# Grouping the 512-wide and the 256-wide matmuls of a turned product in a decoder block

## The chip, the cores and the metric

The kernel runs on one core of one Trainium2 chip. The metric is the device time in microseconds of one execution. Before the change it is 2248.23 us, the median of three runs (2248.22 to 2249.44).

## What is computed

One decoder block on 256 tokens of 2048 features, in float32: a half-step SwiGLU feed-forward net (5632 hidden features), a mixing stage with retention heads and sliding-window heads, cross-attention into 256 memory tokens, a second half-step feed-forward net and a final norm. Cut to what matters:

```python
h = h + 0.5 * swiglu(rms_norm(h, g1), w_gate1, w_up1, w_down1)
n = rms_norm(h, gm) @ w_in                      # queries, keys, values, gates
h = h + concat(retention(n), sliding_window(n)) @ w_out
h = h + cross_attention(rms_norm(h, gx), rms_norm(mem, gme), wq, wkv, wo)
h = h + 0.5 * swiglu(rms_norm(h, g2), w_gate2, w_up2, w_down2)
out = rms_norm(h, gf)
# swiglu(x, g, u, d) = (silu(x @ g) * (x @ u)) @ d
```

Nearly all of the work is the products with weight matrices.

## The kernel before

**Products in halves.** Every float32 operand of a product is written as the sum of a high and a low half in the format `fp32r` (the helper `halves`, lines 70 to 73: ScalarE copies the high half, VectorE subtracts it to get the low one). A product is then three products of halves: high by high, high by low, low by high.

**Two kinds of product.** A plain product holds 128 tokens in TensorE's array and streams 512 (once 256) weight columns past them: `by_tokens` (lines 196 to 203) issues three matmuls per tile of 128 rows through `three` (lines 359 to 363), all of one width. A *turned* product holds a 128x128 tile of the weights in the array and streams the tokens: `by_weights` (lines 205 to 215). Its inputs are blocks `x` of `[128, 4, 2, 256]`: four tiles of 128 features, each as its high and its low half for 256 tokens. For one tile `k` and one half `f` of the unit's 256 output columns it issues two matmuls. The wide one (line 214) holds the weights' high half and streams both halves of `x` in one pass of 512 columns. The narrow one (line 215) holds the weights' low half and streams the high half of `x`, 256 columns, into the first 256 columns of the same bank. Each matmul has a weight load of its own. `acc` is `[128, 2, 512]`: the index `f` chooses one of two banks.

**The stream.** All weight products stand in one list of units (`Unit`, line 129), each a group of 256 or 512 output columns; `run_stream` (line 171) cuts them into steps. A step of a turned product is one block of 512 rows: 4 tiles x 2 halves x 2 matmuls, 16 matmuls. The feed-forward gate and up products, the first down product, the retention queries and keys, `w_out` and cross-attention's queries, keys and output are turned. The other products are plain. A unit of 2048 rows has four turned steps; the units of the first down product have six and five. The first step of a unit opens its accumulation (`start`), the last one closes it (`stop`); in the last tile of the last step the narrow matmul goes first (lines 211 and 212), so that the wide one closes the bank.

**What sets the order.** The instructions are written out step by step. Before each step `run_due` issues small tasks that fell due (norms, attention scores, transposes), and `prepare` keeps the weights three steps ahead (`LOOKAHEAD`, line 30): SyncE issues the load of two steps' weights at once into one of three buffers (`load`, line 147), ScalarE makes the high half `wh` and VectorE the low half `wl` (`split`, line 152) in one of four buffers each. The first eight steps alternate between two units, and their loads are issued ahead of the loop. When a unit's last step is through, its `done` function reads the accumulator.

Of the kernel before, what the change touches and what calls it, by code (L numbers as in the profile page):

```python
# [17 lines left out]
P = 128  # L18
S = 256
# [18 lines left out]
def decoder_block(ctx: ExitStack, tc: tile.TileContext, a: dict, out: bass.AP):  # L38
    nc = tc.nc
# [14 lines left out]
    def blk(dt=F32R):  # L54
        """Four tiles of 128 features by 256 tokens, each as its high and its low half."""
        return work.tile([P, 4, 2, S], dt, tag="blk", name=nm("blk"), bufs=13)
# [13 lines left out]
    def halves(hi, lo, src):  # L70
        """src as the exact sum of two short halves."""
        copy(hi, src)
        nc.vector.tensor_tensor(lo, src, hi, ALU.subtract)  # L73
# [18 lines left out]

    # ------------------------------------------------------------------
    # The stream of weight products, with small tasks between its steps.
    # A product either holds the tokens in the array and gives [tokens, 512 columns], or (turned)
    # holds the weights in it and gives [256 columns, tokens], as two parts still to be added.
    st = {}
    units = []
    tasks = []
# [5 lines left out]
    def when(ready, delay, fn):  # L105
        """fn after a delay, and once ready() holds."""
        def attempt():
            if ready():
                fn()
            else:  # L110
                later(1, attempt)
        later(delay, attempt)
# [16 lines left out]
    class Unit:  # L129
        """One group of n output columns of a product with w, laid out in pieces of 1024 per partition."""  # L130

# [5 lines left out]
        def steps(self):  # L137
            """(unit, block, its tiles of 128 rows, piece of w, first, last)"""
            per = 1024 // self.n
            out = [  # L140
                (self, b, range(i * per, (i + 1) * per), b * (4 // per) + i)
                for b in self.blocks
                for i in range(4 // per)
            ]
            return [x + (i == 0, i == len(out) - 1) for i, x in enumerate(out)]
# [13 lines left out]
    def pin():  # L159
        """Keeps each engine's instructions so far in the order in which they were written."""  # L160
        prev = {}
        for ins in nc.cur_bb.bb.instructions:
            if ins.engine in prev:
                tc.add_manual_dep(
                    ins, prev[ins.engine].name,
                    mybir.DependencyInfo(mybir.DependencyClass.NoSync, mybir.DependencyReason.DATA),
                    reason="program order",
                )
            prev[ins.engine] = ins

    def run_stream():
# [24 lines left out]
        def by_tokens(u, acc, x, wh, wl, ks, t, first, last):  # L196
            ts = slice(t * P, (t + 1) * P)
            o = acc[:, t, : u.n]
            for i, k in enumerate(ks):
# [3 lines left out]
                )  # L203

        def by_weights(acc, x, wh, wl, first, last):
            for k in range(4):
                for f in range(2):
                    fs = slice(f * P, (f + 1) * P)
                    both, main = acc[:, f, :], acc[:, f, :S]
                    if last and k == 3:  # L210
                        nc.tensor.matmul(main, wl[:, k, fs], x[:, k, 0, :], start=False, stop=False)  # L211
                        nc.tensor.matmul(both, wh[:, k, fs], x[:, k, :, :], start=False, stop=True)  # L212
                    else:
                        nc.tensor.matmul(both, wh[:, k, fs], x[:, k, :, :], start=first and k == 0, stop=False)  # L214
                        nc.tensor.matmul(main, wl[:, k, fs], x[:, k, 0, :], start=False, stop=False)  # L215

# [37 lines left out]

    # ------------------------------------------------------------------
    def turn(src):
        """Transposes src(t, kk) [128 tokens, 128] into two banks of [128, 2, 256]."""
        tp = [tmp_ps() for _ in range(2)]
        for kk in range(4):
            for t in range(2):  # L260
                nc.tensor.transpose(
                    tp[kk // 2][:, (kk % 2) * S + t * P : (kk % 2) * S + (t + 1) * P], src(t, kk), ident
                )
        return tp

    def split_turned(tp, gcol):
        """The exact halves of a turned block, each feature times its gain where there is one."""
        x = blk()
        for b in range(2):
            v = tp[b].rearrange("p (k s) -> p k s", k=2)  # L270
            if gcol is None:
                ks = slice(2 * b, 2 * b + 2)
                halves(x[:, ks, 0, :], x[:, ks, 1, :], v)
            else:
                gained(x[:, 2 * b : 2 * b + 2], v, gcol + 2 * b)
        return x

    def gained(x, v, gcol):
        """x = the exact halves of v, each feature times its gain."""
        for k in range(v.shape[1]):  # L280
            g = gains[:, gcol + k : gcol + k + 1]
            copy(x[:, k, 0, :], v[:, k, :], scale=g)
            nc.vector.scalar_tensor_tensor(x[:, k, 1, :], v[:, k, :], g, x[:, k, 0, :], ALU.mult, ALU.subtract)  # L283

    class Norm:
        """Blocks of a normed and split input [features, tokens], made as the blocks of its source come.

        The blocks lack 1 / rms: the results are multiplied by it, per token."""

# [7 lines left out]
        def block(self, b, src):  # L297
            """src: the block's tiles, [128, n, 256] each."""
            x = blk()
            k = 0  # L300
# [5 lines left out]
        def stat(self, src):  # L306
            """Adds the squares of a block to the sums."""
            for v in src:
# [11 lines left out]
        def finish(self):  # L320
            """1 / rms of the tokens, on the partitions."""
            tp = tmp_ps()
# [11 lines left out]
        def spread(self):  # L334
            """The same along the free axis, on every partition."""
            tp = tmp_ps()
# [15 lines left out]
    def total(acc):  # L352
        """The sum of the two parts of a turned product, [128, 2, 256]."""
        x = t2k().rearrange("p (f s) -> p f s", f=2)
# [4 lines left out]
    def three(o, ah, al, bh, bl, start, stop):  # L359
        """o += the product of a sum of halves with another."""  # L360
        nc.tensor.matmul(o, ah, bh, start=start, stop=False)  # L361
        nc.tensor.matmul(o, ah, bl, start=False, stop=False)  # L362
        nc.tensor.matmul(o, al, bh, start=False, stop=stop)  # L363

    # ------------------------------------------------------------------
    def add_to_h(j, acc, factor):
        """Adds 256 features of a turned product to h."""
        v = hT[j // 2][:, 2 * (j % 2) : 2 * (j % 2) + 2, :]
# [5 lines left out]
    def to_h(w, lhs, factor, blocks, norm=None, then=None):  # L374
        """h += factor * (a product with w), and the blocks of the norm that follows."""
        def done(acc, j):
# [47 lines left out]

    # ------------------------------------------------------------------
    n1 = Norm(G_FFN1, "n1")
# [26 lines left out]

    # ------------------------------------------------------------------
    # Retention and sliding-window heads.
    mixT = {}

    def rope(x, t, nh, dst):
        """dst = x [128 tokens, nh, 64] rotated."""
        c, s1, s2 = (  # L460
# [38 lines left out]
    def swa_group(g, t, heads, q, probs):  # L499
        """Scores of some heads for one half of the tokens, and their softmax.  # L500

        The queries' halves lie one above the other and the keys stand twice, so that one pass
        gives (qh + ql) kh and, next to it, (qh + ql) kl."""
        nh = len(heads)
# [196 lines left out]

    # ------------------------------------------------------------------
    # Output projection; the memory's keys and values; cross-attention.
    nxa = Norm(G_XA, "nxa")
# [22 lines left out]
    def put_done(norm, dst, i, f, then=None):  # L727
        """A turned product times 1 / rms, split into its halves, as part of a block."""
        def done(acc):
# [93 lines left out]

    # ------------------------------------------------------------------
    # The last block of products gives [tokens, features]; so does its input then have to be.
    h = []
# [74 lines left out]
def _tables():  # L901
    """Rotary, mask and decay tables: they depend on shapes alone."""
    f = np.float32
# [27 lines left out]
def _pieces(w, n):  # L931
    """w [K, N] as [N / n groups of columns, pieces, 128 rows, 1024]: the pieces in the order in which they are used."""
    k = 1024 // n
# [5 lines left out]
def _turned(x):  # L939
    """x [tokens, features] as [4 blocks * 128 features, 4, tokens]."""  # L940
    return x.T.reshape(4, 4, P, S).transpose(0, 2, 1, 3).reshape(4 * P, 4, S)
# [39 lines left out]
```

## Time and profile before

| | |
|---|---|
| median of three runs | 2248.23 us |
| profiled execution, first to last instruction | 2248.1 us |
| TensorE matmuls, busy share of the span | 12310, 99% |
| matmuls of turned products (lines 211 to 215) | 9600 |
| VectorE, ScalarE busy share | 61%, 48% |
| DMA, mean | 185 GB/s |

The times of the rows come from one profiled execution, and its span is within 0.2 us of the median, so the two can be compared directly. The end of a matmul is modelled in the profile, and a matmul's stated duration overlaps that of the next one. What a matmul costs in a stream is the distance from its start to the next start.

### The profile page before, as it was taken

What the parts mean: (1) busy time and instruction counts of PE and PEld (TensorE: products, weight loads), DVE (VectorE), ACT (ScalarE), POOL (GpSimd) and SP (SyncE); (2) the same over time, 40 slices, a digit from 0 to 9 for tenths busy, and PEclk for the clock granted to TensorE, in tenths of its full rate; (3) what the DMA queues carried; (4) which work ended last, traced back from release to release, by engine and by line L of the source; (5) the groups of instructions that cost most, each with busy time, mean ns of one, the idle gap of its engine ahead of it and who ended that gap; (6) DMA issues with size and microseconds to landing.
All of it is one profiled execution on the core that took longest, in us unless ns stands there. A gap on an engine that the chain in (4) does not pass through costs nothing.

```text
span 2248.1 us, 29814 instructions
## 1 busy us (share of the span) xinstructions
PE 2235.6 (99%) x12310; PEld 1932.7 (86%) x12310; DVE 1381.9 (61%) x1676; ACT 1089.8 (48%) x1371; POOL 13.6 (1%) x17
## 2 busy tenths in 40 slices
PE   9999999999999999999999999999999999999998
PEld 8888888888888888888888888888888888888887
DVE  6656555556566678876765565665656545565554
ACT  5544444444445465545544554555444433444443
POOL 0000000000000000000000000000000000000000
PEclk9999999999999999999999999999999999999999
DMA  7555555555555554445655544455555555555563
GB/s 267 179 185 186 187 186 189 188 187 188 186 197 187 197 169 151 169 167 189 205 186 189 189 167 150 163 185 177 188 187 188 187 188 197 179 187 187 191 216 135
DMA packets 109576, 415.64 MB, mean 185 GB/s; under 512 B 7040, under 2 KB 7040, under 8 KB 109312
## 3 DMA queue, kind: packets, MB, share of 16 engines
q1 hardware_dynamic: 109296, 413.70, 53.8%
q8 instruction: 96, 1.57, 0.3%
q14 instruction: 40, 0.33, 0.0%
q10 hardware_dynamic: 144, 0.05, 0.0%
HBM read 411.62 MB, written 2.10 MB: 184 GB/s over the span
## 4 chain that ended last, share of the span: by engine, by line
PE 98%; DVE 1%; issue 0%; DMA 0%; ACT 0%; SPq 0%; ACTq 0%; POOLq 0%; POOL 0%
PE acc L214 47%; PE acc L215 24%; PE acc L363 7%; PE acc L362 7%; PE acc L361 7%; PE acc L212 3%; PE acc L211 2%; PE tmp L361 0%; PE tmp L363 0%; PE tmp L362 0%; PE tmp L513 0%; DMA wf<-in_ffn_w_gate 0%; PE tmp L539 0%; PE tmp L326 0%; PE tmp L633 0%
## 5 line engine op out<-in xcount | busy, mean ns | idle before, releaser
L214 PE MATMUL acc<-blk,wh 128*128 128x512 f32 x4512 | 1599.3, 398 | 2.8 <-DVE blk L283 2.8
L73 DVE TENSOR_TENSOR wl<-wf,wh 128x1024 fp32r<-128x1024 f32 (+1 forms) x773 | 943.8, 1222 | 621.1 <-ACT wh L68 616.0
L215 PE MATMUL acc<-blk,wl 128*128 128x256 f32 x4512 | 1267.1, 281 | 0.0
L68 ACT ACTIVATE wh<-wf 128x1024 fp32r<-128x1024 f32 (+1 forms) x773 | 816.7, 1057 | 779.1 <-PE acc L214 509.7
L214 PEld LDWEIGHTS acc<-blk,wh 128*128 128x128 f32 x4512 | 848.0, 188 | 201.4 <-DVE blk L283 3.2
L215 PEld LDWEIGHTS acc<-blk,wl 128*128 128x128 f32 x4512 | 853.2, 189 | 6.1 <-DVE wl L73 0.3
L361 PE MATMUL acc<-wh,blk 128*128 128x512 f32 (+1 forms) x704 | 271.6, 386 | 0.0
L362 PE MATMUL acc<-wl,blk 128*128 128x512 f32 (+1 forms) x704 | 270.8, 385 | 0.0
L363 PE MATMUL acc<-wh,blk 128*128 128x512 f32 (+1 forms) x704 | 270.7, 384 | 0.0
L68 ACT ACTIVATE t2k<-acc 128x512 f32<-128x512 f32 x144 | 86.1, 598 | 267.2 <-PE acc L212 265.3
L356 DVE TENSOR_TENSOR t2k<-acc,t2k 128x512 f32<-128x512 f32 x112 | 77.5, 692 | 128.9 <-ACT t2k L68 128.9
L363 PEld LDWEIGHTS acc<-wh,blk 128*128 128x128 f32 x704 | 132.3, 188 | 26.3
L362 PEld LDWEIGHTS acc<-wl,blk 128*128 128x128 f32 x704 | 132.4, 188 | 25.7
L361 PEld LDWEIGHTS acc<-wh,blk 128*128 128x128 f32 x704 | 132.3, 188 | 25.8 <-DVE blk L855 0.2
L212 PE MATMUL acc<-blk,wh 128*128 128x512 f32 x288 | 107.6, 396 | 0.0
L211 PE MATMUL acc<-blk,wl 128*128 128x256 f32 x288 | 81.4, 283 | 0.0
L350 DVE TENSOR_TENSOR t2k<-t2k,rows 128x512 f32<-128x512 f32 x104 | 71.8, 692 | 3.3
L212 PEld LDWEIGHTS acc<-blk,wh 128*128 128x128 f32 x288 | 54.5, 189 | 6.8
L211 PEld LDWEIGHTS acc<-blk,wl 128*128 128x128 f32 x288 | 54.2, 188 | 7.1
L68 ACT ACTIVATE blk<-t2k 128x512 fp32r<-128x512 f32 (+1 forms) x66 | 40.9, 622 | 12.5 <-DVE t2k L350 8.5
L371 DVE TENSOR_TENSOR h<-h,t2k 128x512 f32<-128x512 f32 x32 | 22.2, 692 | 39.2 <-ACT t2k L68 39.2
L73 DVE TENSOR_TENSOR blk<-t2k,blk 128x512 fp32r<-128x512 f32 (+1 forms) x66 | 44.2, 673 | 0.0
(132 smaller groups left out, 691.9 us busy)
## 6 DMA issues: line engine op xcount, KB each, us to landing
wf<-in_ffn_w_gate SPq DMA_DIRECT2D x86, 1024.0 KB, 4.9
wf<-in_ffn_w_up SPq DMA_DIRECT2D x86, 1024.0 KB, 4.9
wf<-in_ffn_w_down SPq DMA_DIRECT2D x84, 1024.0 KB, 4.9
wf<-in_w_in_rqk SPq DMA_DIRECT2D x16, 1024.0 KB, 4.9
wf<-in_w_in_rvg SPq DMA_DIRECT2D x16, 1024.0 KB, 4.8
wf<-in_w_out SPq DMA_DIRECT2D x16, 1024.0 KB, 5.0
wf<-in_xa_wk SPq DMA_DIRECT2D x16, 1024.0 KB, 4.8
wf<-in_xa_wv SPq DMA_DIRECT2D x16, 1024.0 KB, 4.9
```

Source lines behind the costliest of these rows:

```text
L68: return nc.scalar.activation(dst, src, AF.Copy, **kw)
L73: nc.vector.tensor_tensor(lo, src, hi, ALU.subtract)
L211: nc.tensor.matmul(main, wl[:, k, fs], x[:, k, 0, :], start=False, stop=False)
L212: nc.tensor.matmul(both, wh[:, k, fs], x[:, k, :, :], start=False, stop=True)
L214: nc.tensor.matmul(both, wh[:, k, fs], x[:, k, :, :], start=first and k == 0, stop=False)
L215: nc.tensor.matmul(main, wl[:, k, fs], x[:, k, 0, :], start=False, stop=False)
L350: nc.vector.tensor_tensor(x, x, r, ALU.mult)
L356: nc.vector.tensor_tensor(x, acc[:, :, :S], x, ALU.add)
L361: nc.tensor.matmul(o, ah, bh, start=start, stop=False)
L362: nc.tensor.matmul(o, ah, bl, start=False, stop=False)
L363: nc.tensor.matmul(o, al, bh, start=False, stop=stop)
L371: nc.vector.tensor_tensor(v, v, x, ALU.add)
```

## The change

Only `by_weights` does something new. (The diff also takes out comments and docstrings, which is left out here.) In a step the eight wide matmuls stand together (`main_pass`), and so do the eight narrow ones (`low_pass`). Which group goes first changes from step to step, through the flag `wide_first`, so that a step begins with the kind with which the one before it ended; the first step of a unit always begins with the wide ones (they open the accumulation) and the last always ends with them. Within a group the order is tile by tile, and within a tile the two banks in turn.

```diff
+        wide_first = [True]
+
         def by_weights(acc, x, wh, wl, first, last):
-            for k in range(4):
-                for f in range(2):
-                    fs = slice(f * P, (f + 1) * P)
-                    both, main = acc[:, f, :], acc[:, f, :S]
-                    if last and k == 3:
-                        nc.tensor.matmul(main, wl[:, k, fs], x[:, k, 0, :], start=False, stop=False)
-                        nc.tensor.matmul(both, wh[:, k, fs], x[:, k, :, :], start=False, stop=True)
-                    else:
-                        nc.tensor.matmul(both, wh[:, k, fs], x[:, k, :, :], start=first and k == 0, stop=False)
-                        nc.tensor.matmul(main, wl[:, k, fs], x[:, k, 0, :], start=False, stop=False)
+            wide = first or (wide_first[0] and not last)
+            wide_first[0] = not wide
+
+            def main_pass(closing):
+                for k in range(4):
+                    for f in range(2):
+                        nc.tensor.matmul(
+                            acc[:, f, :], wh[:, k, f * P : (f + 1) * P], x[:, k, :, :],
+                            start=first and k == 0, stop=closing and k == 3,
+                        )
+
+            def low_pass():
+                for k in range(4):
+                    for f in range(2):
+                        nc.tensor.matmul(
+                            acc[:, f, :S], wl[:, k, f * P : (f + 1) * P], x[:, k, 0, :], start=False, stop=False
+                        )
+            if wide:
+                main_pass(False)
+                low_pass()
+            else:
+                low_pass()
+                main_pass(last)
```

The number of matmuls, of weight loads, of DMAs and of all other instructions stays as it is.

## Rows read from the trace of the kernel before

**Rows 1.** Page, part 1: busy time of each engine, share, instructions.
```profile
PE 2235.6 (99%) x12310; PEld 1932.7 (86%) x12310; DVE 1381.9 (61%) x1676; ACT 1089.8 (48%) x1371; POOL 13.6 (1%) x17
```

**Rows 2.** Page, part 4: the chain that ended last, by engine.
```profile
PE 98%; DVE 1%; issue 0%; DMA 0%; ACT 0%; SPq 0%; ACTq 0%; POOLq 0%; POOL 0%
```

**Rows 3.** Waits of matmuls and weight loads: us in total, times, longest.
```profile
PE acc L214 <- DVE blk L283: 2.8, 1, 2.8
...
PEld acc L214 <- DVE blk L283: 3.2, 2, 3.0
...
PEld acc L215 <- DVE wl L73: 0.3, 1, 0.3
```

**Rows 4.** Page, part 5: groups of matmuls and a weight load; busy, mean ns.
```profile
L214 PE MATMUL acc<-blk,wh 128*128 128x512 f32 x4512 | 1599.3, 398 | 2.8 <-DVE blk L283 2.8
...
L215 PEld LDWEIGHTS acc<-blk,wl 128*128 128x128 f32 x4512 | 853.2, 189 | 6.1 <-DVE wl L73 0.3
...
L212 PE MATMUL acc<-blk,wh 128*128 128x512 f32 x288 | 107.6, 396 | 0.0
```

**Rows 5.** Three stretches of turned products: window, length, matmuls (x), clock, DMA share.
```profile
100.00:700.00 600.00, 600.00 (x3409) 522.37 (x3408) 349.14 (x355) 276.00 (x308) 0.00 (x0) 1.00 0.55 188
...
1560.00:1770.00 210.00, 210.00 (x1191) 182.29 (x1191) 126.17 (x130) 100.75 (x113) 0.00 (x0) 1.00 0.55 184
1910.00:2130.00 220.00, 220.00 (x1248) 191.02 (x1247) 130.66 (x135) 103.96 (x116) 0.00 (x0) 1.00 0.55 187
```

**Rows 6.** Timeline of TensorE: one early pair, then neighbouring units; start, us, what.
```profile
96.09 0.28 PE L215 MATMUL acc<-blk,wl 128*128 128x256 f32 x1
96.20 0.40 PE L214 MATMUL acc<-blk,wh 128*128 128x512 f32 x1
96.44 0.28 PE L215 MATMUL acc<-blk,wl 128*128 128x256 f32 x1
...
316.04 0.39 PE L212 MATMUL acc<-blk,wh 128*128 128x512 f32 x1
316.27 0.39 PE L214 MATMUL acc<-blk,wh 128*128 128x512 f32 x1
316.49 0.28 PE L215 MATMUL acc<-blk,wl 128*128 128x256 f32 x1
...
333.22 0.40 PE L214 MATMUL acc<-blk,wh 128*128 128x512 f32 x1
...
349.06 0.28 PE L215 MATMUL acc<-blk,wl 128*128 128x256 f32 x1
349.18 0.28 PE L211 MATMUL acc<-blk,wl 128*128 128x256 f32 x1
...
349.88 0.39 PE L214 MATMUL acc<-blk,wh 128*128 128x512 f32 x1
```

**Rows 7.** Timeline, a plain product: its first matmul, and the one behind its last.
```profile
1774.53 0.39 PE L361 MATMUL acc<-wh,blk 128*128 128x512 f32 x1
...
1905.11 0.39 PE L214 MATMUL acc<-blk,wh 128*128 128x512 f32 x1
```

**Rows 8.** Timeline, attention scores: first narrow matmul, and the one behind the last.
```profile
1322.06 0.28 PE L361 MATMUL tmp<-blk,blk 128*128 128x256 f32 x1
...
1324.94 0.40 PE L214 MATMUL acc<-blk,wh 128*128 128x512 f32 x1
```

**Rows 9.** Page, part 5: the weights' halves; busy, mean ns, idle before, releaser.
```profile
L73 DVE TENSOR_TENSOR wl<-wf,wh 128x1024 fp32r<-128x1024 f32 (+1 forms) x773 | 943.8, 1222 | 621.1 <-ACT wh L68 616.0
...
L68 ACT ACTIVATE wh<-wf 128x1024 fp32r<-128x1024 f32 (+1 forms) x773 | 816.7, 1057 | 779.1 <-PE acc L214 509.7
```

**Rows 10.** Timeline, the first step of the stream.
```profile
8.52 1.67 DVE L283 SCALAR_TENSOR_TENSOR blk<-h,gains,blk 128x256 fp32r<-128x256 f32 x4
...
10.49 0.63 PE L214 MATMUL acc<-blk,wh 128*128 128x512 f32 x1
...
11.13 0.63 PE L214 MATMUL acc<-blk,wh 128*128 128x512 f32 x1
```

## The prediction

> **What bounds the kernel now.** I read the page first. TensorE's matmuls are busy 99% of the span, and no other engine is above 61% [rows 1]. The chain of waits says that this is no accident of averaging: 98% of the chain that ended last lies on TensorE [rows 2]. The waits close the case: in the whole execution turned products wait 2.8 us for a block of input at the very start, and their weight loads 3.2 us for blocks and 0.3 us for a low half [rows 3]. So nothing feeds TensorE late, and the time is the sum of what each matmul takes in its stream. There are 4512 + 288 = 4800 pairs of a wide and a narrow matmul in turned products [rows 4]; line 212 is the wide one of the last tile.
>
> The durations in rows 4 (398 ns) overlap and can't be added up. I therefore count starts. In three long stretches that hold nothing but turned products, 3409 + 1191 + 1248 = 5848 matmuls stand in 1030 us, 176.1 ns each, **352.3 ns a pair**, with the clock at 1.00 [rows 5].
>
> The timeline then shows that this is a mean of two rhythms. Between 316.27 and 333.22 us, 48 pairs take 16.95 us, 353.1 ns each. Between 333.22 and 349.88 us, the next 48 pairs of the same kind take 16.66 us, 347.1 ns each [rows 6]. The instructions, engines and shapes are the same; the alternating stream simply falls into a slower or a faster rhythm after each disturbance, and mostly into the slower one.
>
> Streams of one width show a single rhythm. A plain product issues 576 wide matmuls in 1905.11 - 1774.53 = 130.58 us: **226.7 ns** each [rows 7]. The scores of cross-attention issue 24 narrow ones in 2.88 us: **120.0 ns** each [rows 8]. Both have a fresh weight load per matmul and accumulate, as the turned product does. Their sum is 346.7 ns, which is the faster of the two rhythms: there, neither kind pays for its neighbour. In the slower one a pair pays 353.1 - 346.7 = 6.4 ns more for the mixture.
>
> **The change part by part.**
>
> *The grouping.* It removes nothing and adds nothing: 4800 wide and 4800 narrow matmuls remain, each with its load. What it moves is neighbours. Of 16 transitions in a step nearly all are now from like to like, and one is mixed (the flag lets a step begin with the kind that ended the last one). If like follows like at the prices of rows 7 and 8, a pair costs 346.7 in place of 352.3 ns: 5.6 x 4800 = **26.9 us saved**. The trace doesn't show a long run of one width in a turned product, so this is bounded from both sides. The nearest rows are the borders of two units, where wide follows wide at 0.23 us and the next narrow one comes 0.22 us later, and narrow follows narrow at 0.12 us [rows 6]. If every wide one cost 231 ns (between the rounded 0.23 and the 0.226 behind it) and every narrow one 119, a pair would be 350 ns and the gain 2.3 x 4800 = 11 us. At the other end nothing in the trace undercuts 346.7 in a steady stream, and a gain beyond 27 + 3 us would need it. I take 346.7: in rows 6 the wide one at the border takes 0.23 and its follower 0.22, which together is two times 226, and rows 7 and 8 are steady over hundreds and dozens of matmuls.
>
> *The mixed transitions.* One in each of the 600 steps, in turn wide to narrow and narrow to wide. In the slower rhythm a mixed pair costs 6.4 ns extra; 300 such pairs are **2 us**, and that is taken off the gain. It could be nothing or twice that.
>
> *Banks.* Consecutive matmuls now go to the two banks in turn, where a wide and its narrow one shared a bank. Plain products stay in one bank for six matmuls and then change, and hold 226.7 ns over all of them [rows 7]. I cost it at nothing; a price would show as wide runs above 227 ns.
>
> *The low halves of the weights.* A step that begins narrow needs its low half at once, 0.23 us earlier than now; a step that begins wide needs it 8 x 0.227 = 1.8 us after its start, 1.6 us later than now. At 300 steps with no slack at all the price would be 70 us. What covers it: halves are made three steps ahead, 3 x 16 x 0.176 = 8.4 us, and take 1.06 + 1.22 us; ScalarE spends 509.7 us waiting for TensorE to give a buffer free [rows 9], so the halves are early. The only wait for a low half in the whole trace is 0.3 us [rows 3]. Nothing. If the cover went, TensorE would wait on VectorE in every step that begins narrow.
>
> *The fourth tile of a block.* A wide run needs both halves of the last tile after 6 x 0.227 = 1.36 us instead of 6 x 0.347 = 2.08 us. Where a block is fresh that could cost up to 0.7 us; some 50 blocks would be 36 us with no slack. But the only real wait for a block is the first [rows 3]. There TensorE still runs at about half its later pace, a pair every 0.64 us, and VectorE makes the four tiles in 1.67 us, 0.42 us apart [rows 10]. Wide matmuls at half pace need a new tile every 2 x 2 x 0.227 = 0.9 us, so VectorE stays ahead. Nothing, up to 1 us.
>
> *Buffers and transfers.* In a step that ends wide the high half is given back at its end as now; in one that ends narrow, 1 us sooner. The load queue isn't touched, and DMA engines are 55% busy in the stretches [rows 5]. At 1.2% more speed nothing there becomes late.
>
> The sum, against the profiled span of 2248.1 us, which is the median within 0.2 us: 2248.2 - 26.9 + 2 = **2223 us**. About 0.2% is what a measurement of this kernel can tell from no change, that is 4.5 us.
>
> **A rule beside the rows.** Narrow matmuls in a row have no wide one behind which a weight load could hide. A load is recorded at 189 ns [rows 4], longer than a narrow matmul, yet narrow ones run at 120 ns with a load each [rows 8]: loads don't bound them at more than that. The Trainium skill, "TensorE: Matmul & The Clock Gate", section "LDWEIGHTS (loading the stationary operand)", prices a load by its columns at 1.2 GHz, which is about 107 ns as an estimate; this agrees with the 120 ns of the trace as an upper limit.
>
> **The rivals.**
>
> *No change.* The slower rhythm could belong to the turned product (its operands, its two banks) and not to the mixture. Then wide runs keep the extra 6.4 ns, a pair stays near 352 to 353 ns, and the time is 2248 us. The same result comes if the program's scheduler interleaves the groups again. Against it: the very same instructions run at 347.1 ns for 48 pairs in a row [rows 6]. 8%. The same page, section "Back-to-back issue gap", gives a matmul's spacing alone from its own columns plus 2.5 ns; by that no order costs anything and the answer is this rival, but its 216 ns for 512 columns is not what this trace has, 226.7.
>
> *Half the gain.* Wide runs at 231, narrow ones at 119, as worked out above from rows 6: 2248 - 11 = 2237 us. 13%.
>
> *Slower.* In the slower rhythm an early wide matmul steps by 0.24 us and the narrow one before it by 0.11 [rows 6]: of the 353.1 ns some 236 belong to the wide one (an estimate; the rows are rounded to 0.01 us) and 117 to the narrow one. Should the wide one keep that price from its operands, and the narrow ones, with all eight loads back to back, lose their share of the wide one's time and go to 120, then a pair is 356 ns: 3.7 x 4800 = 18 us more, 2266 us. It decides once wide runs stand above 352.3 - 120 = 232.3 ns. Against it: the border of units, where a wide one in front of a wide one is already below that. 5%.
>
> **How the numbers follow.** The forecast, 2223 us, has 74%: rows 7 and 8 are the same kind of instruction in a long run, and their sum is met by a rhythm of the turned product itself. Half the gain 13%, no change 8%, slower 5%. Faster by over 0.2% is the first two, 0.87; the same 0.08; slower 0.05. The range begins at 2217 (27 us and some more from stalls that go) and ends at 2239, which takes in half the gain; it leaves out the last two rivals and a part of the tails.
>
> **What would show it.** In the changed kernel's timeline, wide runs should step by 226 to 227 ns and narrow ones by 120, a step of 16 should take 2.77 us instead of 2.82 in all stretches, and the stretches of turned products should hold one matmul per 173.5 ns. Waits of matmuls should stay a few us. It is wrong if runs of one width show a rhythm of their own (231 or more), if weight loads of narrow matmuls begin to wait for the low half, or if TensorE waits for blocks at the start of units.

## The result, and the profile after

The changed kernel takes 2230.44 us, the median of four runs (2230.02 to 2231.3), beside 2248.84 us for the kernel before (four runs). The ratio is 0.992 with a 95% interval of 0.9906 to 0.9934: faster, by 18.4 us. The forecast was 2223 us, a gain of 25 us; the sign held, and a quarter of the gain was missing.

The page of the changed kernel (line 215 is now every wide matmul of a turned product, line 223 every narrow one):

```profile
span 2229.5 us, 29693 instructions
PE 2217.2 (99%) x12310; PEld 1937.9 (87%) x12310; DVE 1371.2 (62%) x1676; ACT 1082.8 (49%) x1371; POOL 12.1 (1%) x17
...
PE 98%; DVE 1%; issue 0%; DMA 0%; ACT 0%; SPq 0%; ACTq 0%; POOLq 0%; POOL 0%
...
L215 PE MATMUL acc<-blk,wh 128*128 128x512 f32 x4800 | 1153.6, 391 | 2.8 <-DVE blk L299 2.8
...
L223 PE MATMUL acc<-blk,wl 128*128 128x256 f32 x4800 | 628.1, 283 | 0.0
```

The instructions are the same 12310 matmuls, still 98% of the chain, as in [rows 1, 2]. The waits of matmuls and of weight loads in the changed kernel:

```profile
PE acc L215 <- DVE blk L299: 2.8, 1, 2.8
...
PEld acc L223 <- ACT blk L68: 0.5, 2, 0.3
```

The wait for the first block is as long as before [rows 3], and the narrow matmuls' loads wait 0.5 us in total. So nothing became late: the difference lies in the spacing of matmuls. Three stretches of turned products (window, length, TensorE's busy time and matmuls first, clock and DMA share near the end) show it:

```profile
100.00:700.00 600.00, 600.00 (x3448) 530.13 (x3447) 350.62 (x363) 278.92 (x314) 0.00 (x0) 1.00 0.55 191
1545.00:1750.00 205.00, 205.00 (x1178) 181.10 (x1178) 122.85 (x129) 97.45 (x111) 0.00 (x0) 1.00 0.55 190
1895.00:2110.00 215.00, 215.00 (x1237) 189.99 (x1237) 128.06 (x133) 102.64 (x116) 0.00 (x0) 1.00 0.55 190
```

3448 + 1178 + 1237 = 5863 matmuls in 1020 us are 174.0 ns each, 347.9 ns a pair, against 352.3 in [rows 5]. The timeline shows the runs themselves (start, us, what; neighbours of one line are merged, so a row is a run):

```profile
1938.21 3.82 PE L215 MATMUL acc<-blk,wh 128*128 128x512 f32 x16
1941.86 2.08 PE L223 MATMUL acc<-blk,wl 128*128 128x256 f32 x16
1943.78 3.82 PE L215 MATMUL acc<-blk,wh 128*128 128x512 f32 x16
```

Sixteen wide matmuls start in 1941.86 - 1938.21 = 3.65 us, 228.1 ns each, and sixteen narrow ones in 1.92 us, 120.0 each. At the pure prices of [rows 7, 8] a round of both would take 16 x 346.7 = 5.547 us; it takes 5.57. About 20 ns a round are lost (from the unrounded starts of the trace). They arise at the changes: the first five wide matmuls of a run step by 228 to 236 ns and the other eleven by 226 to 227, 27 ns too many in all, and the first narrow one behind a wide one steps by 113 ns in place of 120, which gives some 7 of them back.

### The profile page after: what moved, and what is told of

It is laid out like the page before. It is cut to its first block, busy times and chain, and to the rows that moved or that the text cites. A ratio compares the mean times of both kernels' runs of the same rounds, so it can differ in the third digit from the quotient of the medians.

```text
span 2229.5 us, 29693 instructions
## 1 busy us (share of the span) xinstructions
PE 2217.2 (99%) x12310; PEld 1937.9 (87%) x12310; DVE 1371.2 (62%) x1676; ACT 1082.8 (49%) x1371; POOL 12.1 (1%) x17
## 4 chain that ended last, share of the span: by engine, by line
PE 98%; DVE 1%; issue 0%; DMA 0%; ACT 0%; SPq 0%; ACTq 0%; POOLq 0%; POOL 0%
PE acc L215 49%; PE acc L223 26%; PE acc L377 7%; PE acc L379 7%; PE acc L378 7%; PE tmp L377 0%; PE tmp L378 0%; PE tmp L379 0%; DMA wf<-in_ffn_w_gate 0%; PE tmp L529 0%; PE tmp L555 0%; PE tmp L342 0%; PE tmp L649 0%; DVE wl L73 0%; PE tmp L853 0%
## 5 line engine op out<-in xcount | busy, mean ns | idle before, releaser
L215 PE MATMUL acc<-blk,wh 128*128 128x512 f32 x4800 | 1153.6, 391 | 2.8 <-DVE blk L299 2.8
L215 PEld LDWEIGHTS acc<-blk,wh 128*128 128x128 f32 x4800 | 880.7, 188 | 172.5 <-DVE blk L299 3.1
L223 PEld LDWEIGHTS acc<-blk,wl 128*128 128x128 f32 x4800 | 618.1, 191 | 24.7 <-ACT blk L68 0.5
L223 PE MATMUL acc<-blk,wl 128*128 128x256 f32 x4800 | 628.1, 283 | 0.0
L68 ACT ACTIVATE blk<-tmp 128x512 fp32r<-128x512 f32 (+3 forms) x57 | 25.9, 470 | 26.9 <-DVE blk L73 15.9
L424 DVE TENSOR_TENSOR t2k<-t2k,t2k 128x512 f32<-128x512 f32 x44 | 30.1, 685 | 0.0
L68 ACT ACTIVATE blk<-h,gains 128x256 fp32r<-128x256 f32 x64 | 28.1, 496 | 1.1 <-DVE h L388 1.1
L299 DVE SCALAR_TENSOR_TENSOR blk<-h,gains,blk 128x256 fp32r<-128x256 f32 x64 | 27.5, 480 | 0.0
```

Of the source, the lines that this page charges most:

```text
L68: return nc.scalar.activation(dst, src, AF.Copy, **kw)
L215: nc.tensor.matmul(acc[:, f, :], wh[:, k, f * P : (f + 1) * P], x[:, k, :, :], start=first and k == 0, stop=closing and k == 3,)
L223: nc.tensor.matmul(acc[:, f, :S], wl[:, k, f * P : (f + 1) * P], x[:, k, 0, :], start=False, stop=False)
L424: nc.vector.tensor_tensor(s, s, gated.pop((b, f)), ALU.mult)
```

## The experiments

Theory A said: runs of one width have the pure prices, and each change from narrow to wide and back costs some 20 ns. The rivals said that edges cost nothing (B), or that something other than the mixture makes the surcharge: the weight load behind the narrow matmul (L), or the turned product's operands. One measure serves the runs of this table: the window from 100 to 700 us, which holds nothing but turned products. 600 us over half its matmuls is the price of a pair.

| kernel | time, us | matmuls in 100:700 | ns a pair |
|---|---|---|---|
| before, alternating | 2248.8 | 3409 | 352.0 |
| the change, runs of 16 | 2230.4 | 3448 | 348.0 |
| runs of 8 | 2233.1 | 3443 | 348.5 |
| runs of 2, tile by tile | 2232.4 | 3442 | 348.6 |
| runs of 2, by bank | 2234.6 | 3438 | 349.0 |
| runs of 32 | 2226.3 | 3458 | 347.0 |
| alternating, wide loads halved | 2212.1 | 3488 | 344.0 |
| alternating, narrow loads halved | 2226.4 | 3458 | 347.0 |
| alternating, narrow of 384 columns | 2539.9 | 2905 | 413.1 |
| runs of 16, wide loads halved | 2234.8 | 3436 | 349.2 |

Kernels with one run stand beside runs of the kernel before on their chip, whose medians lie within 1.1 us of 2248.8. Halving a load means that a matmul holds 64 columns of weights in place of 128. It then also gives half as many outputs, and no run separates the two.

### Runs of 8

```diff
-            wide = first or (wide_first[0] and not last)
+            wide = not last
```

> Runs of 8: every step begins with the wide group, only a unit's last step ends with it. Changes from narrow to wide go from about 300 to 600 - 144 = 456. Theory A (runs of one width cost 226.7 and 120 ns, and each change from narrow to wide and back costs 20 ns net, whatever the run length): 156 x 20 ns = 3 us more than the changed kernel, about 2233.5 us. Theory B (a run has its price, edges cost nothing): 2230.4 us. Theory C (a rhythm of its own sets in behind each change and grows with the run): at or below 2230.

Measured: 2233.12 us (four runs, ratio 0.993, 0.9914 to 0.9947), 2.7 us above the changed kernel, as theory A has it. The intervals of the two ratios overlap, so the time alone does not settle it; the spacing in the trace does. Its timeline, where each unit has runs of 8 and of 16:

```profile
1904.81 2.00 PE L215 MATMUL acc<-blk,wh 128*128 128x512 f32 x8
1906.65 1.12 PE L223 MATMUL acc<-blk,wl 128*128 128x256 f32 x8
1907.61 2.00 PE L215 MATMUL acc<-blk,wh 128*128 128x512 f32 x8
```

A round of 8 and 8 takes 2.80 us where pure prices give 2.773. By the unrounded starts it is 2.793: the loss per change is again 20 ns, and does not shrink with the run. The trace has 438 changes from narrow to wide in place of 307 in the changed kernel; 131 of them at 20 ns are 2.6 us.

### Runs of 2

```diff
...
+                closing = last and k == 3
+                for wide in (False, True) if closing else (True, False):
+                    for f in range(2):
...
```

> Runs of 2: for each tile two wide ones, then two narrow ones, 2400 changes from narrow to wide. Theory A with a fixed 20 ns a change: (2400 - 300) x 20 ns = 42 us above the changed kernel, 2272 us. Theory A with a cost that only builds up over a run: between 2224 and 2248 us, a pair at 346.7 to 353 ns. Theory B: 2222 us, a pair at 346.7.

```profile
1920.30 0.63 PE L212 MATMUL acc<-blk,wh 128*128 128x512 f32 x2
1920.77 0.39 PE L216 MATMUL acc<-blk,wl 128*128 128x256 f32 x2
1921.00 0.63 PE L212 MATMUL acc<-blk,wh 128*128 128x512 f32 x2
...
1922.39 0.62 PE L212 MATMUL acc<-blk,wh 128*128 128x512 f32 x2
```

2232.36 us (one run), not 2272. Three rounds take 2.09 us, 348.3 ns a pair, so a change costs only 3 or 4 ns here. At the borders of steps the same kernel has runs of four; there a change costs 13 ns by the starts in the trace. So the loss of 20 ns is built up by a run; with eight of a kind it is there in full. Two of a kind already bring nearly all of the gain, which theory A with a fixed price did not expect.

The other order of runs of 2 asked whether sharing a bank with the neighbour matters:

```diff
+                    for wide in (True, False) if first and k == 0 or f == 0 and not closing else (False, True):
```

> Runs of 2 in another order: wide, narrow on one bank, then narrow, wide on the other. If only the length of the runs counts, a pair costs 349.4 ns as in the other kernel with runs of 2, 2232 us. If it counts whether neighbours share a bank, it differs by some ns a pair, at most back to 352 ns and 2248 us.

2234.56 us and 349.0 ns a pair in the window against 348.6: 0.4 ns a pair, one run each. Banks matter little.

### Halving the load behind a narrow matmul

```diff
-                        nc.tensor.matmul(both, wh[:, k, fs], x[:, k, :, :], start=first and k == 0, stop=False)
+                        m = P if first and k == 0 else 64
+                        nc.tensor.matmul(
+                            acc[:m, f, :], wh[:, k, f * P : f * P + m], x[:, k, :, :],
+                            start=first and k == 0, stop=False,
+                        )
```

> The alternating kernel of before, but the wide matmuls hold only 64 of their 128 weight columns (but for a unit's opening and closing ones), so that half of their outputs is left out; the load that has to fit behind a narrow matmul is half as long. Theory L (the slower rhythm comes from the load of the wide one's weights, which just does not fit behind a narrow matmul): the surcharge goes and the narrow one falls below 120 to about 113, a pair costs 340 to 341 ns, some 4200 pairs by 12 ns, 2197 us. Theory M (mixing the widths costs by itself): pairs stay at 352, 2248 us.

2212.1 us, between the theories. The timeline of one stretch:

```profile
1919.85 0.39 PE L215 MATMUL acc<-blk,wh 128*64 128x512 f32 x1
1920.08 0.28 PE L219 MATMUL acc<-blk,wl 128*128 128x256 f32 x1
1920.19 0.39 PE L215 MATMUL acc<-blk,wh 128*64 128x512 f32 x1
...
1921.21 0.39 PE L215 MATMUL acc<-blk,wh 128*64 128x512 f32 x1
```

Four pairs take 1.36 us, 340 ns each, the price that theory L gave. In other units the same kernel runs slower:

```profile
2040.64 0.39 PE L215 MATMUL acc<-blk,wh 128*64 128x512 f32 x1
...
2042.03 0.39 PE L215 MATMUL acc<-blk,wh 128*64 128x512 f32 x1
```

Four pairs here take 1.39 us; by the unrounded starts they are 346.7 ns each, and about half of the units run at either price. There are again two rhythms 6.7 ns apart, both one notch lower. The lower one is a sum of pure prices again: in the kernel before, attention scores with loads of 64 columns settle at 113.3 ns a step in place of 120.0, and 226.7 + 113.3 = 340.0. So the load, or the outputs halved with it, has a part in it. Halving the load that runs beside the wide matmul instead:

```diff
-                        nc.tensor.matmul(main, wl[:, k, fs], x[:, k, 0, :], start=False, stop=False)
+                        nc.tensor.matmul(
+                            acc[:64, f, :S], wl[:, k, f * P : f * P + 64], x[:, k, 0, :], start=False, stop=False
+                        )
```

> The alternating kernel of before, but the narrow matmuls hold only 64 of their 128 weight columns (half of their outputs is left out), so that the load that runs beside a wide matmul is halved and the one beside a narrow matmul stays whole. Theory L1 (the load beside a narrow matmul makes the slower rhythm): nothing changes, a pair stays near 352 ns, 2248 us. Theory L2 (any shorter load loosens it): the faster rhythm throughout, a pair at 347 ns or less, 2221 us or below. The run with the wide one's load halved gave 344.5 ns a pair and the faster rhythm throughout.

2226.36 us, 347.0 ns a pair: the whole load is recorded at 0.19 us and runs beside a wide matmul that steps by 0.23, and halving it counts all the same. By the starts nearly every unit holds 346.7 ns. Theory L1 falls, as far as one run shows it. (The run with the wide one's load halved was not in one rhythm throughout, as this expectation has it; its 344.0 ns are a mean of two.)

### Giving the load more room

```diff
-                    both, main = acc[:, f, :], acc[:, f, :S]
+                    both, main = acc[:, f, :], acc[:, f, :384]
+                    low = x[:, k, :, :].rearrange("p c s -> p (c s)")[:, :384]
...
-                        nc.tensor.matmul(main, wl[:, k, fs], x[:, k, 0, :], start=False, stop=False)
+                        nc.tensor.matmul(main, wl[:, k, fs], low, start=False, stop=False)
```

> The alternating kernel of before, but the narrow matmuls stream 384 columns in place of 256 (they add a part of the product of low halves, which is otherwise left out). 384 columns at the wide ones' price per column are 170 ns. Theory L: a load fits behind 170 ns, no surcharge, a pair at 397 ns, 2248 + 4800 x 44 ns = 2459 us. Theory M: the surcharge of about 6 ns stays, a pair at 403 ns, 2489 us.

2539.89 us: a miss for both. The window holds this many matmuls:

```profile
100.00:700.00 600.00, 600.00 (x2905) 531.53 (x2904) 295.82 (x298) 231.20 (x257) 0.00 (x0) 1.00 0.47 159
```

That is 413.1 ns a pair, 16 ns above the expectation's 397. No run shows a pure stream of 384 columns; a line through 120.0 and 226.7 ns gives 173.3 as an estimate, a pair at 400.0 and a surcharge of 13 ns. With 50% more columns behind which the load can run, the surcharge did not go; it doubled at the least. That speaks against "the load just does not fit". By the starts most units hold 413.3 ns and a few 406.7: two rhythms 6.7 ns apart once more.

### Runs of 16 with half loads

```diff
+                        m = P if first and k == 0 or closing and k == 3 else 64
                         nc.tensor.matmul(
-                            acc[:, f, :], wh[:, k, f * P : (f + 1) * P], x[:, k, :, :],
+                            acc[:m, f, :], wh[:, k, f * P : f * P + m], x[:, k, :, :],
```

> The changed kernel with wide matmuls of 64 weight columns, but for a unit's opening and closing ones (half of their outputs is left out). If the 28 ns that a wide run loses on its first five matmuls come from weight loads, they go, a pair costs 346.7 ns or less and the time is 2219 us or less. If they come from the change of width alone, they stay: 2230 us.

```profile
1930.02 3.83 PE L216 MATMUL acc<-blk,wh 128*64 128x512 f32 x16
1933.69 2.08 PE L224 MATMUL acc<-blk,wl 128*128 128x256 f32 x16
1935.61 3.83 PE L216 MATMUL acc<-blk,wh 128*64 128x512 f32 x16
```

2234.81 us (one run), slower than with whole loads. Sixteen wide matmuls now take 3.67 us, 229.4 each. A halved load makes an alternating stream quicker and a run of wide ones slower. Both expectations missed. By the starts the first five of a run are no longer dearer than the rest (229.4 ns on average, like the whole run), so their surcharge did go; but the price of all sixteen rose. Behind plain products, where no narrow run stands ahead, a run of eight takes 1.833 us in place of 1.813, so that part is no cost of a change.

### Wide matmuls alone

```diff
-            if wide:
-                main_pass(False)
-                low_pass()
-            else:
-                low_pass()
-                main_pass(last)
+            main_pass(last)
```

> The narrow matmuls are left out (the product with the weights' low half); only wide runs remain. If a wide matmul of a turned product costs 226.7 ns in a pure run, turned products take 4800 x 226.7 ns = 1088 us against 1675 us in the changed kernel, and the time is about 1643 us, more only if loads or halves become late, which the waits would show. If its operands carry a surcharge of their own, the run steps by 231 to 236 ns, 1664 to 1688 us.

Two stretches:

```profile
100.00:300.00 200.00, 200.00 (x884) 165.59 (x883) 171.56 (x175) 136.54 (x151) 0.00 (x0) 1.00 0.82 292
400.00:600.00 200.00, 189.18 (x906) 156.49 (x905) 166.52 (x238) 129.97 (x189) 0.70 (x1) 0.98 0.67 235
```

200 us over 884 matmuls is 226.2 ns (the window cuts through its first and last one), and by the starts in the trace every step in it is 226 or 227 ns. So the turned product's operands and its two banks carry no surcharge; the step "like follows like at the prices of rows 7 and 8" is shown for the wide ones; for the narrow ones the runs of the changed kernel show it, at 120.0. The time, 1681 us in place of 1643, is the other half of the expectation: in the second stretch TensorE is busy for 189 of 200 us and waits for halves and blocks, and DMA moves 292 GB/s in the first.

### The two rhythms of the alternating stream

In the kernel before, the last tile of a unit is turned round (narrow first). Without that:

```diff
-                    if last and k == 3:
-                        nc.tensor.matmul(main, wl[:, k, fs], x[:, k, 0, :], start=False, stop=False)
-                        nc.tensor.matmul(both, wh[:, k, fs], x[:, k, :, :], start=False, stop=True)
-                    else:
-                        nc.tensor.matmul(both, wh[:, k, fs], x[:, k, :, :], start=first and k == 0, stop=False)
-                        nc.tensor.matmul(main, wl[:, k, fs], x[:, k, 0, :], start=False, stop=False)
+                    nc.tensor.matmul(both, wh[:, k, fs], x[:, k, :, :], start=first and k == 0, stop=False)
+                    nc.tensor.matmul(main, wl[:, k, fs], x[:, k, 0, :], start=False, stop=last and k == 3)
```

> The alternating kernel of before without the turned-round last tile of a unit: wide, narrow, wide, narrow from a unit's start to its end and across the border of units. Theory R (two rhythms, and a stream stays in the one it is in until something other than an alternating pair comes by; the turned-round tile is such a thing): each stretch of turned products holds one rhythm from its first pair to its last, 353.3 or 346.7 ns a pair. The long feed-forward stretches begin in the slower one in the trace of before, so the whole comes to about 2250 us. Theory S (the slower rhythm is just what units begin with, and it wears off): pairs drift to 346.7, below 2248 us, at best 2221.

2246.57 us (one run). The long window, and two stretches of one kind of product, with the same instructions:

```profile
100.00:700.00 600.00, 600.00 (x3397) 520.32 (x3397) 347.69 (x353) 273.42 (x306) 0.00 (x0) 1.00 0.55 187
1560.00:1770.00 210.00, 210.00 (x1214) 185.15 (x1213) 127.74 (x133) 100.93 (x114) 0.00 (x0) 1.00 0.55 188
1910.00:2130.00 220.00, 220.00 (x1245) 190.76 (x1244) 130.69 (x134) 103.35 (x117) 0.00 (x0) 1.00 0.56 188
```

The window gives 353.3 ns a pair, the stretches 346.0 and 353.4 (a matmul more or less at a window's edge is 0.3 ns). The first stretch is in the faster rhythm from its first undisturbed pair to its last, the second in the slower one, and the longest, from 60.9 us on, in the slower one for 1975 pairs. Theory R holds: the rhythm is a state that persists. By the unrounded starts the slower one is a cycle of three pairs: the wide ones step by 236, 233 and 241 ns and the narrow ones behind them by 113, 117 and 120, 1060 ns in all.

Can it be set? In five single steps the third tile was turned round, so that the turn comes right behind a narrow matmul that steps by 113 to 114 ns:

```diff
...
-                    if last and k == 3:
+                    if turn and k == 2:
...
+                turn = at == 17 or (not before.turned and before.n == 512 and u not in skip)
```

> The kernel without the turned-round last tile, but with one tile turned round (narrow before wide, pairs 4 and 5) in five single steps: at the start of the longest stretch (step 17) and in the first turned step behind four of the plain products, where the run without any turned tile fell into the slower rhythm. Theory R (the rhythm is a phase that such a turn can flip, when it comes right behind a wide at 236 and a narrow at 113): about 1975 + 640 + 80 + 48 pairs go from 353.3 to 346.7 ns, 18 us off 2246.6, 2228 to 2229 us, level with or a little under the changed kernel. Theory Q (the rhythm hangs on something else in those stretches, their weights or their place in memory): no change, 2247 us.

> The changed kernel once more, on the same chip and beside the same runs of the kernel before, to set the run with turned pairs against: 2230.4 us as before, within 1 us.

Four of the five turns flip the rhythm in the profiled execution. At the start of the last stretch (lines 211 and 212 are the turned tile):

```profile
1902.94 0.40 PE L214 MATMUL acc<-blk,wh 128*128 128x512 f32 x1
1903.18 0.28 PE L215 MATMUL acc<-blk,wl 128*128 128x256 f32 x1
1903.29 0.28 PE L211 MATMUL acc<-blk,wl 128*128 128x256 f32 x1
...
1910.00:2130.00 220.00, 220.00 (x1263) 193.61 (x1262) 134.68 (x139) 105.70 (x120) 0.00 (x0) 1.00 0.57 192
```

The narrow matmul ahead of the turn steps by 0.11 us, and the stretch behind holds 1263 matmuls in place of 1245. That speaks against theory Q for these four. The fifth turn, at the start of the longest stretch, missed in this execution:

```profile
62.56 0.40 PE L214 MATMUL acc<-blk,wh 128*128 128x512 f32 x1
62.80 0.28 PE L215 MATMUL acc<-blk,wl 128*128 128x256 f32 x1
62.92 0.28 PE L211 MATMUL acc<-blk,wl 128*128 128x256 f32 x1
...
100.00:700.00 600.00, 600.00 (x3399) 520.30 (x3398) 348.54 (x354) 272.99 (x305) 0.00 (x0) 1.00 0.55 187
```

Here the narrow one ahead of the turn steps by 0.12 us: the turn met the cycle of three at another point, and the stretch stayed in the slower rhythm. The nine runs of this kernel fall into two groups, five at 2227.2 to 2228.2 us, within 1 us of what theory R had, and four at 2241.9 to 2242.5; the profiled one is of the second. Their distance of 14 us is what 1975 pairs at 6.6 ns would make (13 us). That the first group is the one in which this turn took is inferred from that sum; no profile of it was taken. The changed kernel beside it took 2229.05 us (four runs, 2228.2 to 2231.9; ratio 0.9913, 0.9896 to 0.9929), 1.4 us below its first measurement, a little outside the expected 1 us. So an alternating stream can be as quick as a grouped one, but only by luck of phase; the grouped one shows no such second group in its eight runs.

### Runs of 32

If runs of 16 lose 20 ns a change, longer runs should save. In units of four steps, but the first two: wide of steps 1 and 2, narrow of steps 1 to 4, wide of steps 3 and 4.

```diff
...
+            elif part == 0:
+                refill()
+                main_pass(False)
+                kept.append(low_pass)
+            elif part == 1:
+                main_pass(False)
+                kept.pop()()
+                refill()
+                low_pass()
+            elif part == 2:
+                refill()
+                low_pass()
+                kept.append(lambda: main_pass(False))
+            else:
+                low_pass()
+                kept.pop()()
+                refill()
+                main_pass(True)
...
```

> The changed kernel with runs twice as long in all units of four steps (but the first two): wide of steps 1 and 2, narrow of steps 1 to 4, wide of steps 3 and 4, so that a unit has one change from narrow to wide in place of two. Halves stay where they are, but the preparing of the next ones stands up to a step later. Theory A, as the runs of 8 and of 16 bear it out (20 ns a change from narrow to wide and back): some 126 changes fewer, 2.5 us less than the changed kernel's 2229 to 2230.4, 2227 us. Rival: the halves come late now that they are prepared later; waits of weight loads for them appear and the time is level or above 2230.

2226.34 us (four runs, 2225.9 to 2227.44; ratio 0.9902, 0.9886 to 0.9919), the fastest here of the kernels that compute the whole block, and within 1 us of the expectation. Its runs, and the waits of its weight loads for blocks:

```profile
1915.18 7.44 PE L213 MATMUL acc<-blk,wh 128*128 128x512 f32 x32
1922.46 4.00 PE L221 MATMUL acc<-blk,wl 128*128 128x256 f32 x32
1926.29 7.44 PE L213 MATMUL acc<-blk,wh 128*128 128x512 f32 x32
...
PEld acc L213 <- DVE blk L325: 2.2, 1, 2.2
...
PEld acc L221 <- ACT blk L68: 0.7, 3, 0.3
```

A round of 32 and 32 takes 11.11 us; pure prices give 11.093. By the unrounded starts the round is 20 ns above them, as with 16, now spread over twice as many pairs; the trace has 181 changes from narrow to wide in place of 307. Halves did not come late. It was not run side by side with the changed kernel. Their runs of 2228.2 to 2231.9 and 2225.9 to 2227.4 us do not overlap, but the intervals of their ratios do, so what shows the gain is the spacing rather than the time.

## Why the prediction was right, and where it was short

- **What bounds the kernel**: right. No wait of a matmul or a weight load grew by more than 0.5 us, and the time follows the spacing of matmuls.
- **The grouping, 26.9 us**: right in price. Narrow ones in a run step by 120.0 ns and undisturbed wide ones by 226 to 227; wide matmuls alone run at that price too. The sign "wide runs should step by 226 to 227" came true for eleven of sixteen.
- **The mixed transitions, "2 us, it could be nothing or twice that"**: this is the mis-sized term. It was taken from the slower rhythm, 6.4 ns a mixed pair. A change behind a run of eight or more costs about 20 ns; 307 of them are 6.1 us. The alternating stream cannot show this price, since it only builds up over a run (4 ns behind two of a kind, 13 behind four). The runs of 8 and of 32 bear it out in both directions: 2.7 us more and 2.7 to 4 us less than the changed kernel.
- **The rest, some 2 us**: the forecast took the price of three stretches without small tasks for all 4800 pairs. By the starts in the traces a pair went from 353.1 to 350.1 ns in the 1424 pairs from the mixing stage to the start of the second feed-forward net, where small tasks stand between the steps, against 353.1 to 348.0 in the last 1264. The traces also show where this lies: of what turned matmuls take above the pure prices, 3.2 us in this part (2.7 in the kernel before) stand on the some 340 that come just ahead of another kind of matmul or within eight behind one. Grouping does not touch these. In all, turned matmuls stood 30.3 us above the pure prices before the change and 11.2 after it: 6.1 for the changes, 3.2 here, and 1.9 in the first 112 pairs.
- **Banks, low halves, fourth tile, buffers, each at nothing**: right; the waits of the changed kernel show next to none of them (0.5 us for blocks), and banks made 0.4 ns a pair in the runs of 2.
- **The rivals**: "no change" and "slower" fall with the wide-only run. "Half the gain" named 350 ns a pair and 2237 us, and the time, 2230.4, lies midway between it and the forecast. Its reason was another one: wide ones at 231 throughout and narrow ones at 119. A run of 16 has 228.4 and 119.5 as means, from its first few matmuls alone. The time stayed within the range because the range had been drawn to take in this rival, and not because the price of a change was foreseen.
- **The rules beside the rows**: the Trainium skill, "TensorE: Matmul & The Clock Gate", section "Back-to-back issue gap", gives the spacing by a matmul's own columns that the prediction cites, but as that of an isolated matmul; for a stream of loads and matmuls it says that both set the spacing. By the formula alone order would cost nothing; the runs disagree, since order alone moved the time by 18 to 22 us. Its price of a load was cited as no bound beyond 120 ns. That stands, but the runs with halved loads suggest that a load's length enters a pair's price even where it is hidden.

That like follows like at the pure prices, and what a change costs, is shown. The cause beneath stays open. Mixed widths lock into rhythms 6.7 ns apart; halved loads shift them, more columns in the narrow matmul worsen them, and a run's first five wide matmuls step by more behind a narrow run. No single one of the mechanisms tried explains all of these.

## What to carry to other kernels

When an engine never waits, count starts, not durations, and compare the stream's price per item with that of pure streams elsewhere in the trace: the gap between 352 and 347 ns was readable before anything was changed. Price the edges of a regrouping by a run that has them, or leave them a wide bound: here they took 4 us more than a mean over an alternating stream suggested. And prefer an order whose price does not hang on a phase: the runs of one alternating kernel lay in two groups 14 us apart, most likely by whether one turned tile took.

## What was not expected of the hardware

- An alternating stream of 512- and 256-column matmuls holds one of two rhythms, 346.7 or 353.3 ns a pair, for up to 1975 pairs, and a single tile in the other order (two pairs) can flip it: four of five did.
- Halving the columns of a weight load that is hidden, and the outputs with them, made an alternating stream quicker (352.0 to 344.0 or 347.0 ns a pair) and a run of 16 wide matmuls slower (3.65 to 3.67 us).
- 512 and 384 columns in alternation cost 413 ns, more above their pure price (13 to 16 ns, an estimate) than 512 and 256 (6.6 ns at the most).
- The rhythms of every alternating kernel that shows two lie 6.7 ns apart: 340.0 and 346.7 ns with the wide one's load halved, 346.7 and 353.3 as it was, 406.7 and 413.3 with 384 columns.
